# Output weight halved ahead of time: a two-layer decoder step on one core

## The chip, the cores and the metric

The kernel runs on one core of a Trainium2 chip. A core has five engines that run their own instruction streams: TensorE (PE in the profile, with its weight loads as PEld), VectorE (DVE), ScalarE (ACT), GpSimd (POOL) and SyncE (SP), which here only issues DMA transfers. The time is device microseconds (us) of one execution. One execution with the hardware profiler on gives the profile and the trace.

## The reference, cut to what matters

One inference step of a decoder with two layers, a Mamba-2 SSD layer and a multi-head latent attention (MLA) layer, for a prompt of 1024 tokens and 8 sample sequences of 8 tokens each, all in float32, model width 1024. The change is in the MLA layer.

```
def mla_sample_attn(q_nope, q_pe, ckv, kpe, pool_ckv, pool_kpe, layer, page_table, w_uk, w_uv):
    q_lat = absorb(q_nope, w_uk)
    stats = latent_partial(q_lat, q_pe, ckv, kpe, causal)
    def page_step(carry, pt):
        page = latent_partial(q_lat, q_pe, pool_ckv[layer, pt], pool_kpe[layer, pt], None)
        return merge_partial(carry, page), None
    (_, l, acc), _ = lax.scan(page_step, stats, page_table.T)
    return latent_out(l, acc, w_uv)

def mla_output(o, gate, w_out):
    gated = o.reshape(b, t, MLA_WIDTH) * jax.nn.silu(gate.astype(F32))
    return jnp.einsum('bte,ed->btd', gated.astype(gate.dtype), w_out)
```

The gate is a part of the layer's input projection. Each sample sequence has 2048 cached tokens in pages (a latent of 256 and a rotary key of 32 per token). After `mla_output` come the residual sum and a final RMSNorm. `w_out` is 1024 x 1024.

## The kernel before

Matrix products that must keep float32 accuracy are made from halves: a value x is held as hi, its rounding to the matmul's input type, and lo = x - hi, and a product is three matmuls, hi*hi, hi*lo, lo*hi. `split` (line 125) makes them: ScalarE casts hi, VectorE (or GpSimd) subtracts for lo.

The MLA layer goes through these stages.

- Gates (`gate_block`, line 970, eight blocks b of 128 columns, three token pieces each): weight block loaded by `load_w` (line 316), split by ScalarE and GpSimd, 24 matmuls a piece, ScalarE's Silu into `gt`, stored to DRAM as `g_d`. `gather_kpe` and `page_rows` run between them; the gathered rotary keys go to DRAM as two 2 MB stores `kpe_d`.
- Latent and query projections (`mla_kv`, `mla_cq`, `mla_q`).
- Prompt attention, 16 heads (`mla_heads`, line 1466). In the last head the sample attention's first eleven steps (`FLOW`) are mixed in, and `preload` (line 1582) loads two of the eight 128-row blocks of the output weight.
- Sample attention with the output projection (`mla_sample`, line 1844). `Sample.flow` (line 1790) walks over 32 steps n, called pages here: one step treats 512 cached tokens of one sequence (four pages of the cache). A step transposes the next cache rows (`turn`, matmuls ct), transposes the last probabilities (`turn_p`, pt), makes the scores (`scores`, seven matmuls sc, the last from the rotary keys tk), takes their maximum (mx, nm) and exponential (P) (`softmax`, line 1640) and multiplies the last probabilities with the cache rows (`values`, matmuls o, accumulated in ac). `halves` (line 1706) splits the next cache rows: ScalarE casts kvh, GpSimd subtracts kvl. Cache rows pgr come by GpSimd's indirect DMA four steps ahead, rotary keys tk by SP two steps ahead.
- `MlaOut` (line 1869) holds the output projection. `pieces` is a generator that yields after half an output tile's first matmuls; `flow` calls it from step 8 on, so that its matmuls fill TensorE between the pages.

The weight blocks kk are taken in the order `WORD`. Six more blocks are loaded by SP three at a time (`weight`, line 1879), and `weight_split` (line 1884) makes their halves in steps 2 to 7:

```
WSP = (2, 3, 4, 4, 5, 6, 6, 7)
WENG = (2, 0, 2, 0, 2, 0, 2, 0)
```

`WSP` gives the step of each block, `WENG` who subtracts, GpSimd (2) or VectorE (0): one cast of 128 x 1024 on ScalarE and four subtractions of 128 x 256. For each output tile `load` fetches the gated attention output `og` and `split` cuts it into oh and ol, one tile ahead.

The order of TensorE's and GpSimd's instructions in the head and sample stages is as written. ScalarE's, VectorE's and SP's order is made when the program is built, by a planner with its own model of times: it may move an instruction ahead of others that are not ready. `issue_after(x)` keeps the instructions written inside it behind x on x's engine. Each engine runs its queue in order, so an instruction that waits holds those behind it.

Of the kernel before, what the change touches and what calls it, by code (L numbers as in the profile page):

```python
# [16 lines left out]
D = 1024  # L17
# [950 lines left out]


def gate_block(k, wp, raws, b):  # L970
    with k.tc.issue_after(k.gts[5].ins) if b in (3, 4) else nullcontext():
        ws = kslices(load_w(k, wp, k.I["mla_w_in"][0][:, 800 + 128 * b : 928 + 128 * b], 8, 128, "wg", 3, raws,
                            eng=k.nc.gpsimd, sub=4), 8)
    gt = wp.tile([128, T], F32, tag="gt", name=f"gt{b}", bufs=2)

    def ev(ci, t0, n, p):
        k.gts.append(k.nc.scalar.activation(gt[:, t0 : t0 + n], p[:, :n], AF.Silu))
# [18 lines left out]
def mla_in(k, right, mid):  # L996
    tc, nc, I = k.tc, k.nc, k.I
    k.g_d = k.dram.tile([8, 128, T], F32, name="g_d")
    with ExitStack() as st:
# [17 lines left out]
        k.kvs = [k.cm.tile([128, 2, 64], F32R, name=f"kvs{x}") for x in "hl"]  # L1017
        gates = (None for b in range(2, 8) for _ in gate_block(k, wg, rw, b))
        with open_pool(tc, name="kg", bufs=1, side="right") as kg:
# [20 lines left out]
        wcq = load_cw(k, wq, rw, 0, 512, "cw")  # L1040
        mla_kv(k, sp, wkv)
        wk.close()
# [5 lines left out]

def mla_kv(k, sp, ws):
    nc, I = k.nc, k.I  # L1050
# [7 lines left out]
    for i, (t0, m) in enumerate(TILES):  # L1058
# [39 lines left out]
        if i < 8:  # L1098
            kh, kl = k.kT
            split(k, kh[64:96, t0 : t0 + m], kl[64:96, t0 : t0 + m], p[64:96, 256 : 256 + m])  # L1100


# [363 lines left out]
def mla_heads(k, hd, sm, early, st):  # L1466
# [8 lines left out]
    for h in range(MH):  # L1475
# [19 lines left out]
        for t in range(12):  # L1495
# [8 lines left out]
            if h + 1 == MH and t == 0:  # L1504
                sm.preload()
            if len(held) > LEAD:
# [45 lines left out]
class Sample:  # L1552
# [28 lines left out]

    def preload(self):
        k = self.k
        self.pre = ExitStack()
        pp = self.pre.enter_context(open_pool(k.tc, name="pre4", bufs=1))
        self.wraw = {}
        for kk in WORD[:2]:
            self.wraw[kk] = pp.tile([128, D], F32, name=f"w5p{kk}")
# [18 lines left out]
    def late_open(self, st):  # L1607
        self.pre.close()
# [10 lines left out]
    def load_tk(self, n):  # L1619
        k, nc = self.k, self.k.nc  # L1620
        tk = self.ep.tile([96, 4, 256], F32R, tag="tk", name=f"tk{n}", bufs=2)
        for j in range(3):
            src = k.kpe_d[j % 2][:, :, 128 * n : 128 * n + 256].rearrange("r c x -> c r x")
            with k.tc.issue_after(k.lastq.ins):
                nc.sync.dma_start(tk[32 * j : 32 * j + 32].bitcast(F32), src)
        for j in range(2):
# [13 lines left out]
    def softmax(self, name, s, n, old):  # L1640
# [9 lines left out]
        l = self.small(name, "l4", 1, 4)  # L1650
        nc.scalar.activation(P[:, :n], s, AF.Exp, bias=nm, scale=SCALE, accum_out=l)
        f = None
# [39 lines left out]
    def turn(self, n, c):  # L1692
# [6 lines left out]
        tl = self.ep.tile([128, 512], F32R, tag=f"cTl{c}", name=f"cTl{n}_{c}", bufs=2)  # L1699
        a = nc.scalar.copy(th, pt)  # L1700
        b = nc.vector.tensor_tensor(tl, pt, th.bitcast(F32), op=ALU.subtract)
        if self.out:
            self.out.pins = a, b
        self.cT[n, c] = (th, tl)
# [85 lines left out]
    def flow(self):  # L1790
        N = len(self.items)
        for n in range(-1, N + 1):
# [9 lines left out]
            if t:  # L1802
                self.turn(n + 1, 1)
                yield
            parts = [WORD[WSP.index(n) + x] for x in range(WSP.count(n))] if out else []
# [29 lines left out]
            if out:  # L1835
                if n in MORE:
                    next(out.fill, None)
                if n + 1 == OUT0[0]:
                    next(out.fill)
                    self.k.nc.sync.dma_start(out.fw, self.k.I["final_norm_w"].partition_broadcast(128))  # L1840
            yield


def mla_sample(k, sm, flow):
    with ExitStack() as st:
        psum = st.enter_context(open_pool(k.tc, name="ps4", bufs=1, space=PS))
        out = MlaOut(k, st, psum)
        sm.open(st, psum, out)
        out.raw = sm.wraw
        for kk in WORD[2:5]:  # L1850
            out.weight(kk)
        out.fill = fill = out.pieces(range(8))
        next(fill)
        for _ in flow:
            if not hasattr(sm, "accT") and not any(kk in out.raw for kk in WORD[:2]):
                sm.late_open(st)
        last = None
# [11 lines left out]
class MlaOut:  # L1869
    def __init__(self, k, st, psum):  # L1870
        tc, nc, I = k.tc, k.nc, k.I
# [3 lines left out]
        self.fw = sp.tile([128, D], F32, name="fw")  # L1875
        self.raw = {}
        self.ws = [[self.wp.tile([128, D], F32R, name=f"w5{x}{kk}", bufs=1) for x in "hl"] for kk in range(8)]

    def weight(self, kk):
        k, nc, wp = self.k, self.k.nc, self.wp  # L1880
        self.raw[kk] = self.sp.tile([128, D], F32, tag="h5", name=f"w5r{kk}", bufs=3)
        WQ(nc).dma_start(self.raw[kk], k.I["mla_w_out"][0][kk * 128 : kk * 128 + 128])

    def weight_split(self, kk, half):
        hi, lo = self.ws[kk]
        raw = self.raw[kk]
        nc, x = self.k.nc, WENG[WORD.index(kk)]
        if not half:
            with self.k.tc.issue_after(self.pins[0].ins):
                nc.scalar.copy(hi, raw)  # L1890
        for a in range(2 * half, 2 * half + 2):
            s = slice(256 * a, 256 * a + 256)
            with self.k.tc.issue_after(self.pins[1].ins):
                (nc.gpsimd if x & 2 else nc.vector).tensor_tensor(lo[:, s], raw[:, s], hi[:, s].bitcast(F32),
                                                                  op=ALU.subtract)
        if half:
            del self.raw[kk]
            if 2 <= WORD.index(kk) < 5:
                self.weight(WORD[WORD.index(kk) + 3])

    def pieces(self, tiles, src=None):
        k, nc, sp, ws = self.k, self.k.nc, self.sp, self.ws

        def load(i):
            t0, m = TILES[i]
            oh = sp.tile([128, 8, 128], F32R, tag="oh5", name=f"oh5{i}", bufs=2)
            ol = sp.tile([128, 8, 128], F32R, tag="ol5", name=f"ol5{i}", bufs=2)
            g = src
            if i < 8:
                g = sp.tile([128, 8, 128], F32, tag="og5", name=f"og5{i}", bufs=2)  # L1910
                nc.sync.dma_start(g, k.og_d[:, :, t0 : t0 + m].rearrange("b p t -> p b t"))
            return oh[:, :, :m], oh[:, :, 64:] if m == 64 else ol, g, oh

        queue = [load(tiles[0])]
        if tiles[0] == 0:
            yield
        split(k, *queue[0][:3], parts=4 if tiles[0] == 0 else 0)
        if tiles[0] == 0:
            yield
        for n, i in enumerate(tiles):  # L1920
            t0, m = TILES[i]
            oh, ol, _, o2 = queue.pop(0)
# [8 lines left out]
            for hf, c in enumerate(cs):  # L1931
# [3 lines left out]
                for j, _ in enumerate(mm_tok(nc, p, m, nw, [  # L1935
                        (oh[:, kk], ol[:, kk], o2[:, kk], ws[kk][0][:, c], ws[kk][1][:, c]) for kk in WORD])):
                    if j == (7 if src else 11) and nw == 512:
# [142 lines left out]
```

## Time and profile before

| | us |
|---|---|
| median of three runs (lowest, highest) | 1930.48 (1929.45, 1934.53) |
| the profiled execution | 1939.72 |
| its span, first to last instruction | 1937.9 |
| mean granted TensorE clock | 0.994 |
| TensorE busy | 1894.9 |

Slices of the page: TensorE's busy tenths are 9 nearly everywhere; the lower ones are at the change from the first to the second half of the SSD layer (776 to 824 us), at the start of the sample attention, and at the end. A busy TensorE in this profile is not TensorE at its peak, since matmuls overlap; the granted clock tells when it ran slower. Stretches of time are given in us from the span's start. In the list of waits the columns are who waited, for whom, us in total, times and the longest. In a group the number after the bar is busy time, then the mean of one in ns, then idle time before it. In a timeline row the first two numbers are start and duration; a bracket holds the idle time before it and who ended it.

### The profile page before, as it was taken

What the parts mean: (1) busy time and instruction counts of PE and PEld (TensorE: products, weight loads), DVE (VectorE), ACT (ScalarE), POOL (GpSimd) and SP (SyncE); (2) the same over time, 40 slices, a digit from 0 to 9 for tenths busy, and PEclk for the clock granted to TensorE, in tenths of its full rate; (3) what the DMA queues carried; (4) which work ended last, traced back from release to release, by engine and by line L of the source; (5) the groups of instructions that cost most, each with busy time, mean ns of one, the idle gap of its engine ahead of it and who ended that gap; (6) DMA issues with size and microseconds to landing.
All of it is one profiled execution on the core that took longest, in us unless ns stands there. A gap on an engine that the chain in (4) does not pass through costs nothing.

```text
span 1937.9 us, 33631 instructions
## 1 busy us (share of the span) xinstructions
PE 1894.9 (98%) x12023; PEld 1733.7 (89%) x12023; DVE 1209.1 (62%) x2500; ACT 1100.4 (57%) x2525; POOL 828.6 (43%) x1122
## 2 busy tenths in 40 slices
PE   9999999999999999899999999999999999899998
PEld 7999999999999999788788998998888888688887
DVE  5557676767676767755534114567877878766674
ACT  6467566666666766732214314436777777755552
POOL 2447555555655555443004222104333435854551
PEclk9999999999999999999999999999999999989999
DMA  5123323233333332644434342223111112645441
GB/s 166 50 78 90 94 80 100 82 106 87 93 89 92 89 93 88 202 145 172 168 109 127 114 163 86 72 96 92 48 47 43 53 42 82 212 142 155 156 128 39
DMA packets 181088, 202.02 MB, mean 104 GB/s; under 512 B 18829, under 2 KB 147609, under 8 KB 180537
## 3 DMA queue, kind: packets, MB, share of 16 engines
q1 hardware_dynamic: 175864, 180.08, 30.3%
q0 software_dynamic: 4976, 19.66, 3.0%
q8 instruction: 95, 1.56, 0.3%
q14 instruction: 73, 0.59, 0.1%
q10 hardware_dynamic: 80, 0.13, 0.0%
HBM read 146.52 MB, written 53.28 MB: 103 GB/s over the span
## 4 chain that ended last, share of the span: by engine, by line
PE 87%; DMA 4%; ACT 3%; DVE 3%; issue 1%; POOL 1%; SPq 0%; POOLq 0%; DVEq 0%; ACTq 0%
PE pj L86 24%; PE pz L98 7%; PE pq L98 6%; PE pob L98 5%; PE p L98 5%; PE poa L98 3%; PE py L638 3%; PE sc L86 3%; PE o L86 2%; PE sc L1376 2%; PE o L1439 2%; PE o L1441 2%; PE st L1408 2%; DMA M<-acs_d 2%; PE st L1409 2%; PE st L1410 2%
## 5 line engine op out<-in xcount | busy, mean ns | idle before, releaser
L86 PE MATMUL pj<-xl,wih 128*128 128x384 f32 (+1 forms) x768 | 255.4, 333 | 0.0
L86 PE MATMUL pj<-xh,wih 128*128 128x384 f32 (+1 forms) x768 | 252.9, 333 | 0.5 <-ACT raw L512 0.3
L86 PE MATMUL pj<-xh,wil 128*128 128x384 f32 (+1 forms) x768 | 252.9, 329 | 0.0
L1422 POOL TENSOR_TENSOR tl<-P,th 128x384 fp32r<-128x384 f32 (+1 forms) x96 | 90.6, 944 | 232.3 <-ACT P L1420 190.6
L526 DVE SCALAR_TENSOR_TENSOR acc<-raw,vec,acc 128x1112 f32<-128x1112 f32 x96 | 139.9, 1458 | 14.3 <-ACT acc L522 13.4
L98 PE MATMUL pz<-wih,xh 128*128 128x256 f32 x504 | 143.4, 288 | 2.5 <-ACT z L567 2.5
L86 PEld LDWEIGHTS pj<-xh,wih 128*128 128x128 f32 x768 | 143.8, 188 | 1.9 <-ACT xh L273 0.7
L86 PEld LDWEIGHTS pj<-xl,wih 128*128 128x128 f32 x768 | 144.5, 188 | 1.0
L86 PEld LDWEIGHTS pj<-xh,wil 128*128 128x128 f32 x768 | 144.4, 188 | 0.5
L98 PE MATMUL pz<-wil,xh 128*128 128x256 f32 (+1 forms) x504 | 139.6, 283 | 0.0
L1419 ACT ACTIVATE th<-st 128x512 fp32r<-128x512 f32 x192 | 94.6, 493 | 65.9 <-PE st L1415 50.3
L633 ACT ACTIVATE M<-M,tok 128x128 f32<-128x128 f32 (+1 forms) x288 | 91.0, 386 | 67.7 <-DVE M L629 67.2
L98 PE MATMUL pz<-wih,xl 128*128 128x256 f32 x448 | 128.9, 288 | 0.0
L1712 POOL TENSOR_TENSOR kvl<-pgr,kvh 128x256 fp32r<-128x256 f32 x128 | 96.5, 781 | 65.6 <-ACT kvh L1710 65.5
L133 DVE TENSOR_TENSOR wil<-wraw,wih 128x512 fp32r<-128x512 f32 x88 | 74.2, 849 | 40.7 <-ACT wih L127 34.0
L98 PEld LDWEIGHTS pz<-wih,xh 128*128 128x128 f32 x504 | 95.9, 190 | 3.5 <-ACT z L567 2.9
L1420 ACT ACTIVATE P<-st 128x512 f32<-128x512 f32 x192 | 93.5, 487 | 0.0
L98 PEld LDWEIGHTS pz<-wil,xh 128*128 128x128 f32 (+1 forms) x504 | 92.8, 184 | 0.3
L614 POOL TENSOR_TENSOR xdd<-xsT,tok 128x256 f32<-128x256 f32 x64 | 49.9, 779 | 90.2 <-ACT xsT L600 89.7
L98 PEld LDWEIGHTS pz<-wih,xl 128*128 128x128 f32 x448 | 85.3, 190 | 0.5
L1422 DVE TENSOR_TENSOR tl<-P,th 128x512 fp32r<-128x512 f32 x96 | 70.7, 737 | 19.5 <-ACT P L1420 19.3
L127 ACT CAST wih<-wraw 128x512 fp32r<-128x512 f32 x92 | 55.9, 616 | 43.9 <-PE pj L86 28.9
(834 smaller groups left out, 6295.1 us busy)
## 6 DMA issues: line engine op xcount, KB each, us to landing
wraw<-in_ssd_w_in SPq DMA_DIRECT2D x92, 256.0 KB
M<-acs_d SPq DMA_DIRECT2D x64, 256.0 KB
s<-in_state_ssm SPq DMA_DIRECT2D x32, 256.0 KB
y_d<-y SPq DMA_DIRECT2D x64, 128.0 KB
out_s_ssm<-s SPq DMA_DIRECT2D x32, 256.0 KB
wraw<-in_ssd_w_out SPq DMA_DIRECT2D x12, 512.0 KB
q_d<-qt SPq DMA_DIRECT2D x32, 192.0 KB
qp<-q_d SPq DMA_DIRECT2D x8, 768.0 KB
```

The lines of the kernel that those rows point to most:

```text
L86: nc.tensor.matmul(out, a, b, start=(i == 0), stop=(i == n - 1))
L98: nc.tensor.matmul(o, a, b, start=(j == 0), stop=(j == len(ops) - 1))
L127: k.cast = nc.scalar.copy(hi, src)
L133: return (eng or nc.vector).tensor_tensor(lo, src, hi.bitcast(F32), op=ALU.subtract)
L526: last = nc.vector.scalar_tensor_tensor(acc, raw[:, j : j + n], k.convw[j][:, blk : blk + 1], acc, op0=ALU.mult, op1=ALU.add)
L614: nc.gpsimd.tensor_tensor(v3(xdd), v3(xsT), hb(2), op=ALU.mult)
L633: nc.scalar.activation(M[:m, h, :m], M[:m, h, :m], AF.Exp, bias=tk[:, 0, 4 * g + h : 4 * g + h + 1])
L638: nc.tensor.matmul(py[:m, h * 64 : h * 64 + 64], M[:m, h, :m], xsT[:m, h * 64 : h * 64 + 64], start=True, stop=True)
L1419: nc.scalar.activation(th[:, :n], ps[:, :n], AF.Exp, scale=SCALE)
L1420: nc.scalar.activation(P[:, :n], ps[:, :n], AF.Exp, scale=SCALE)
L1422: eng.tensor_tensor(tl[:, :n], P[:, :n], th[:, :n].bitcast(F32), op=ALU.subtract)
L1712: nc.gpsimd.tensor_tensor(rl[:, j], raw[:, j], rh[:, j].bitcast(F32), op=ALU.subtract)
```

## The change

The halves of the output weight are made in the gates' stage: `stage_out`, a generator with sixteen steps, loads half a block (128 x 512), casts hi, subtracts lo, and stores both to a DRAM tensor `w5_d`. One step is taken after each gate piece from the third of block 2 on, sixteen in all. `mla_kv` asks for further steps, of which there are none left then. In the last head two blocks of `w5_d` (both halves, 1 MB each) are preloaded on SP's queue; the other six are loaded one per page in steps 2 to 7 by DMAs that ScalarE issues, each behind the exponential of the step before. `weight_split` and its pins are gone.

In `pieces` two output tiles are loaded at the start and the third when the second is cut; the loads of later tiles, of the residual rows h and of the final norm's weight are issued behind the latest load of rotary keys; the subtractions for ol (four of 128 x 256 a tile) stand behind the latest `nm`, the negated maximum. `accT` and `gs4` are allocated from the start beside the preloaded blocks.

```
-WSP = (2, 3, 4, 4, 5, 6, 6, 7)
-WENG = (2, 0, 2, 0, 2, 0, 2, 0)
+NPW = 2
+WSP = (2, 3, 4, 5, 6, 7)
...
-    k.nc.sync.dma_start(raw, src.rearrange("(k p) e -> p k e", p=128))
+    k.lastload = k.nc.sync.dma_start(raw, src.rearrange("(k p) e -> p k e", p=128))
...
+def stage_out(k, pool):
+    nc = k.nc
+    k.w5_d = k.dram.tile([8, 128, 2, D], F32, name="w5_d")
+    for n in range(16):
+        kk, s = WORD[n // 2], slice(512 * (n % 2), 512 * (n % 2) + 512)
+        t = pool.tile([128, 2, 512], F32, tag="w5s", name=f"w5s{n}", bufs=3)
+        with k.tc.issue_after(k.lastload.ins):
+            nc.sync.dma_start(t[:, 1], k.I["mla_w_out"][0][kk * 128 : kk * 128 + 128, s])
+        nc.scalar.copy(t[:, 0].bitcast(F32R), t[:, 1])
+        nc.vector.tensor_tensor(t[:, 1].bitcast(F32R), t[:, 1], t[:, 0], op=ALU.subtract)
+        nc.sync.dma_start(k.w5_d[kk][:, :, s], t)
+        yield
...
+        stage = stage_out(k, st.enter_context(open_pool(tc, name="w5s", bufs=1)))
...
+        def gate_steps():
+            for b in range(2, 8):
+                for ci, _ in enumerate(gate_block(k, wg, rw, b)):
+                    if b > 2 or ci > 1:
+                        next(stage, None)
+                    yield
...
+        for kk in WORD[:NPW]:
+            self.ws[kk] = pp.tile([128, 2, D], F32R, name=f"w5{kk}")
             with k.tc.issue_after(k.lastq.ins):
-                k.nc.sync.dma_start(self.wraw[kk], k.I["mla_w_out"][0][kk * 128 : kk * 128 + 128])
+                k.nc.sync.dma_start(self.ws[kk].bitcast(F32), k.w5_d[kk])
...
-        nc.scalar.activation(P[:, :n], s, AF.Exp, bias=nm, scale=SCALE, accum_out=l)
+        self.expi = nc.scalar.activation(P[:, :n], s, AF.Exp, bias=nm, scale=SCALE, accum_out=l)
...
-            for kk in parts:
-                out.weight_split(kk, 0)
+            if out and n >= 0:
+                out.weights(n)
             if 0 <= n < N:
                 self.scores(n)
                 self.weigh(n)
-            if parts:
-                out.pins = out.pins[0], self.nmi
-            for kk in parts:
-                out.weight_split(kk, 1)
...
-                    self.k.nc.sync.dma_start(out.fw, self.k.I["final_norm_w"].partition_broadcast(128))
+                    with self.k.tc.issue_after(self.lasttk.ins):
+                        self.k.nc.sync.dma_start(out.fw, self.k.I["final_norm_w"].partition_broadcast(128))
...
+    def weights(self, n):
+        k = self.k
+        for x in range(WSP.count(n)):
+            kk = WORD[NPW + WSP.index(n) + x]
+            with k.tc.issue_after(k.sm.expi.ins):
+                k.nc.scalar.dma_start(self.ws[kk].bitcast(F32), k.w5_d[kk])
...
         def load(i):
+            t0, m = TILES[i]
+            g = sp.tile([128, 8, 128], F32, tag="og5", name=f"og5{i}", bufs=2)
+            with k.tc.issue_after(k.sm.lasttk.ins) if i > 1 else nullcontext():
+                nc.sync.dma_start(g, k.og_d[:, :, t0 : t0 + m].rearrange("b p t -> p b t"))
+            return g
+
+        def halves(i, g):
...
+                nc.scalar.copy(a, g)
+                for j in range(4):
+                    s = slice(2 * j, 2 * j + 2)
+                    with k.tc.issue_after(k.sm.nmi.ins):
+                        nc.vector.tensor_tensor(b[:, s], g[:, s], a[:, s].bitcast(F32), op=ALU.subtract)
...
+            g = [load(0), load(1)]
             yield
+            cut = [halves(0, g.pop(0))]
             yield
...
-            nc.sync.dma_start(h[:m], k.h_d[t0 : t0 + m])
-            if n + 1 < len(tiles):
-                queue.append(load(tiles[n + 1]))
+            with k.tc.issue_after(k.sm.lasttk.ins):
+                nc.sync.dma_start(h[:m], k.h_d[t0 : t0 + m])
...
                 if hf == 0:
                     if n + 1 < len(tiles):
-                        split(k, *queue[0][:3], parts=4 if tiles[n + 1] < 8 else 0)
+                        cut.append(halves(tiles[n + 1], g.pop(0)))
+                    if n + 2 < len(tiles):
+                        g.append(load(tiles[n + 2]))
```

More of the change, by code (lines that the diff above doesn't have):

```diff
@@ L1017, in mla_in @@
         k.kvs = [k.cm.tile([128, 2, 64], F32R, name=f"kvs{x}") for x in "hl"]
-        gates = (None for b in range(2, 8) for _ in gate_block(k, wg, rw, b))
+        def gate_steps():
[4 more added lines that the diff above has]
+                    yield
+        gates = gate_steps()
         with open_pool(tc, name="kg", bufs=1, side="right") as kg:
@@ L1046, in mla_in, with mla_kv @@
         mla_cq(k, sp, wcq)
-def mla_kv(k, sp, ws):
+def mla_kv(k, sp, ws, stage):
     nc, I = k.nc, k.I
@@ L1100, in mla_kv @@
             split(k, kh[64:96, t0 : t0 + m], kl[64:96, t0 : t0 + m], p[64:96, 256 : 256 + m])
+        next(stage, None)
 def mla_cq(k, sp, ws):
@@ L1580, in pt, with preload @@
         return self.psum.tile([128, 512], F32, tag=tag, name=name, bufs=bufs)
-    def preload(self):
+    def preload(self, st):
         k = self.k
[L1584 to L1588, printed above, removed]
+        pp = st.enter_context(open_pool(k.tc, name="pre4", bufs=1))
+        self.ws = {}
+        for kk in WORD[:NPW]:
+            self.ws[kk] = pp.tile([128, 2, D], F32R, name=f"w5{kk}")
             with k.tc.issue_after(k.lastq.ins):
-                k.nc.sync.dma_start(self.wraw[kk], k.I["mla_w_out"][0][kk * 128 : kk * 128 + 128])
+                k.nc.sync.dma_start(self.ws[kk].bitcast(F32), k.w5_d[kk])
     def load_cn(self, b):
@@ L1699, in turn @@
         tl = self.ep.tile([128, 512], F32R, tag=f"cTl{c}", name=f"cTl{n}_{c}", bufs=2)
[L1700 to L1703, printed above, removed]
+        split(k, th, tl, pt)
         self.cT[n, c] = (th, tl)
@@ L1804, in flow @@
                 yield
-            parts = [WORD[WSP.index(n) + x] for x in range(WSP.count(n))] if out else []
-            for kk in parts:
-                out.weight_split(kk, 0)
+            if out and n >= 0:
+                out.weights(n)
             if 0 <= n < N:
@@ L1846, in mla_sample @@
         psum = st.enter_context(open_pool(k.tc, name="ps4", bufs=1, space=PS))
-        out = MlaOut(k, st, psum)
+        out = MlaOut(k, st, psum, sm)
         sm.open(st, psum, out)
-        out.raw = sm.wraw
-        for kk in WORD[2:5]:
-            out.weight(kk)
+        sm.late_open(st)
+        k.sm = sm
         out.fill = fill = out.pieces(range(8))
         next(fill)
-        for _ in flow:
-            if not hasattr(sm, "accT") and not any(kk in out.raw for kk in WORD[:2]):
-                sm.late_open(st)
+        drain(flow)
         last = None
@@ L1875, in __init__ @@
         self.fw = sp.tile([128, D], F32, name="fw")
[L1876 to L1899, printed above, removed]
+        self.ws = dict(sm.ws)
+        for kk in WORD[NPW:]:
+            self.ws[kk] = self.wp.tile([128, 2, D], F32R, name=f"w5{kk}", bufs=1)
+    def weights(self, n):
[4 more added lines that the diff above has]
+                k.nc.scalar.dma_start(self.ws[kk].bitcast(F32), k.w5_d[kk])
     def pieces(self, tiles, src=None):
@@ L1905, in load @@
             t0, m = TILES[i]
+            g = sp.tile([128, 8, 128], F32, tag="og5", name=f"og5{i}", bufs=2)
[4 more added lines that the diff above has]
+            t0, m = TILES[i]
             oh = sp.tile([128, 8, 128], F32R, tag="oh5", name=f"oh5{i}", bufs=2)
             ol = sp.tile([128, 8, 128], F32R, tag="ol5", name=f"ol5{i}", bufs=2)
[L1908 to L1915, printed above, removed]
+            a, b = oh[:, :, :m], oh[:, :, 64:] if m == 64 else ol
+            if src:
+                split(k, a, b, g)
+            else:
+                nc.scalar.copy(a, g)
[3 more added lines that the diff above has]
+                        nc.vector.tensor_tensor(b[:, s], g[:, s], a[:, s].bitcast(F32), op=ALU.subtract)
+            return a, b, oh
+        if src is None:
+            g = [load(0), load(1)]
             yield
-        split(k, *queue[0][:3], parts=4 if tiles[0] == 0 else 0)
-        if tiles[0] == 0:
+            cut = [halves(0, g.pop(0))]
             yield
+        else:
+            cut = [halves(tiles[0], src)]
         for n, i in enumerate(tiles):
             t0, m = TILES[i]
-            oh, ol, _, o2 = queue.pop(0)
+            oh, ol, o2 = cut.pop(0)
             h = sp.tile([128, D], F32, tag="h5", name=f"h5{i}", bufs=3)
-            nc.sync.dma_start(h[:m], k.h_d[t0 : t0 + m])
-            if n + 1 < len(tiles):
-                queue.append(load(tiles[n + 1]))
+            with k.tc.issue_after(k.sm.lasttk.ins):
+                nc.sync.dma_start(h[:m], k.h_d[t0 : t0 + m])
             ss = sp.tile([128, 4], F32, tag="ss5", name=f"ss5{i}", bufs=2)
```

11 lines of the change are left out of this document (5 added, 6 removed).

## The prediction

> **What bounds the kernel now.** I read the page first, then busy time by stretches, then the waits of one stretch, then its timeline by engine.
>
> ```profile
> PE 1894.9 (98%) x12023; PEld 1733.7 (89%) x12023; DVE 1209.1 (62%) x2500; ACT 1100.4 (57%) x2525; POOL 828.6 (43%) x1122
> ...
> 1071.00:1150.00 79.00, 78.77 (x493) 78.33 (x492) 6.99 (x15) 17.98 (x33) 16.62 (x24) 1.00 0.34 127
> 1667.60:1717.70 50.10, 37.52 (x207) 32.83 (x206) 38.14 (x76) 30.90 (x59) 34.71 (x44) 0.83 0.76 242
> 1717.70:1891.50 173.80, 173.80 (x1034) 150.56 (x1033) 111.49 (x244) 93.17 (x204) 90.97 (x114) 1.00 0.43 137
> 1891.50:1937.90 46.40, 38.46 (x233) 33.25 (x231) 23.17 (x60) 12.42 (x29) 7.29 (x11) 0.95 0.10 32
> ```
>
> The first line is busy time of each engine over the span. In the others the columns are the stretch, its length, busy time of PE, weight loads, DVE, ACT and POOL, the granted clock, DMA share and GB/s. TensorE is busy for 98% of the span, so only idle TensorE time and a low clock can be won. The gates (1071 to 1150) and the pages with output tiles between them (1717.7 to 1891.5) leave nothing. The stretch from 1667.6 to 1717.7, pages 3 to 8 of the sample attention, leaves 12.6 us idle, at a clock of 0.83. There stand the splits of the output weight. Who is waited for:
>
> ```profile
> PE pt L1739 <- ACT P L1651: 4.2, 2, 3.8
> PE pt41n L1678 <- ACT P41n L1651: 3.2, 1, 3.2
> PE o L86 <- DVE ac L1760: 3.1, 1, 3.1
> PE o L86 <- DVE pTl L133: 2.0, 2, 1.1
> ...
> 1674.00:1678.00 4.00, 3.04 (x25) 2.91 (x25) 4.00 (x7) 2.31 (x5) 3.81 (x6) 1.00 1.09 370
> 1690.00:1694.00 4.00, 1.72 (x6) 1.45 (x7) 4.00 (x8) 0.00 (x0) 3.81 (x6) 0.65 0.61 201
> 1706.00:1710.00 4.00, 4.00 (x15) 3.42 (x14) 1.95 (x4) 2.78 (x4) 2.81 (x4) 0.50 0.69 254
> ```
>
> All four waits (12.5 us of the 12.6) are for ScalarE or VectorE work of the softmax chain. VectorE is busy for the whole of 1674 to 1678 and 1690 to 1694, and after the idle time TensorE runs at half clock (0.50). What those engines do there beside the attention:
>
> ```profile
> L1894 POOL TENSOR_TENSOR w5l<-w5r,w5h 128x256 fp32r<-128x256 f32 x12 | 9.1, 781 | 0.0
> L1894 DVE TENSOR_TENSOR w5l<-w5r,w5h 128x256 fp32r<-128x256 f32 x12 | 8.7, 775 | 0.0
> L1890 ACT CAST w5h<-w5r 128x1024 fp32r<-128x1024 f32 x6 | 6.1, 1048 | 0.0
> ...
> L1894 DVE TENSOR_TENSOR w5l<-w5p,w5h 128x256 fp32r<-128x256 f32 x4 | 3.9, 1023 | 0.0
> L1894 POOL TENSOR_TENSOR w5l<-w5p,w5h 128x256 fp32r<-128x256 f32 x4 | 2.8, 729 | 2.2 <-PE ct L1697 2.2
> L1890 ACT CAST w5h<-w5p 128x1024 fp32r<-128x1024 f32 x2 | 2.1, 1053 | 0.0
> ```
>
> So 12.6 us of VectorE, 8.2 of ScalarE and 11.9 of GpSimd are splits: of VectorE's 38.14 us a third.
>
> **The splits leave (gain).** What six pages cost without them is bounded by two kinds of page:
>
> ```profile
> 1667.34 0.39 PE L86 MATMUL sc<-tk,qpr 96*128 96x512 f32 x1
> 1672.68 0.39 PE L86 MATMUL sc<-tk,qpr 96*128 96x512 f32 x1
> 1672.91 0.17 PE L86 MATMUL sc41n<-kvsh,qlh 128*128 128x8 f32 x1
> 1673.61 0.37 PE L86 MATMUL o<-kvh,pTh 128*128 128x256 f32 x1
> 1684.74 0.69 PE L1687 MATMUL o41n<-cn,pn 8*128 8x256 f32 x2
> 1725.40 0.39 PE L86 MATMUL sc<-tk,qpr 96*128 96x512 f32 x1
> 1725.63 0.40 PE L98 MATMUL p<-w5h,oh 128*128 128x512 f32 x1
> 1728.39 0.28 PE L86 MATMUL o<-kvh,pTh 128*128 128x256 f32 x1
> 1732.68 0.40 PE L86 MATMUL sc<-tk,qpr 96*128 96x512 f32 x1
> ```
>
> The last score matmul marks a page. From page 9 to 10 TensorE never waits: 1732.68 - 1725.40 = 7.28 us, of which twelve output matmuls take 1728.39 - 1725.63 = 2.76; a page is 4.52 us of TensorE work. That is the floor. From page 2 to 3, where no page has its full share of splits yet, it is 1672.68 - 1667.34 = 5.34 us, TensorE waiting a little for the chain score, maximum, exponential, transpose. Pages 3 to 8 also hold two sets of first scores (1673.61 - 1672.91 = 0.70 each) and one first accumulation (0.69): 2.1 us. So six pages take 6 x 4.52 + 2.1 = 29.2 to 6 x 5.34 + 2.1 = 34.1 us, against 50.1. I take 5.0 a page, 32.1 us: without filler between them the chain stays visible, but page 2 to 3 still holds one cast of 1.05 us. Gain 18.0 us, bounds 16.0 and 20.9. The clock's part is in it, since the floor was measured at full clock, and with gaps under 1 us a page it should stay there. Late next is the same chain, at about 0.5 us a page.
>
> **Weight slices on ScalarE's queue (cost inside that gain, and a risk).** Six triggers stand in ScalarE's order after an exponential. The trace has one trigger of that queue, and on SP both a quick case and a held one:
>
> ```profile
> 1669.94 1.49 SPq L1882 DMA_DIRECT2D w5r<-in_mla_w_out  x3
> 1673.44 3.24 SPq L1625 DMA_DIRECT2D tk<-kpe_dh  x1
> 1933.83 0.56 ACTq L1972 DMA_DIRECT2D out_y_sample<-h  x1
> ```
>
> 0.5 us each, 3 us in all, is less than the 8.2 us of casts that go; I count it as inside the 5.0. The bound above is 3.24 us each, 19.4 in all, what SP's queue was held with the three of the first row and more loads before it. Behind a held trigger wait the cache cast, the transposes' casts and the next exponential, and TensorE for them. I take the low end, since ScalarE's queue would hold one or two slices at a time.
>
> **Bytes.** A slice is 128 x 2 x 1024 x 4 B = 1.05 MB, a page's cache rows 0.52 MB, its rotary keys 0.20: 1.77 MB a page. At the 370 GB/s of the row of 1674 to 1678 that is 4.8 us, under 5.0 but only just. The two output tiles, the final norm's weight and the sample gates (1.8 MB) add 4.9 us once: 6 x 4.8 + 4.9 = 33.7 us, 1.6 above my 32.1. The last slice is wanted only in page 9, so half of this shows: +0.8. The two preloaded halves make one 1.05 MB more at the start of the last head (2.8 us at that rate). Behind it on SP stand page 2's keys (next fence), not used until 1667.34: nothing.
>
> **Output tiles.** Loads move behind the latest keys, subtractions behind the maximum.
>
> ```profile
> 1645.68 1.18 SPq L1625 DMA_DIRECT2D tk<-kpe_dh  x1
> 1678.35 1.05 ACT L127 CAST oh<-og 128x1024 fp32r<-128x1024 f32 x1 [0.74 <-DMA og<-og_d]
> 1687.14 3.55 DVE L131 TENSOR_TENSOR ol<-og,oh 128x256 fp32r<-128x256 f32 x4
> ```
>
> Before, the second tile's four subtractions held VectorE for 3.55 us ahead of the work that TensorE then waited 3.1 us for (the accumulation). Now only the first tile falls in the stretch, its subtractions after page 7's maximum, where half a tile of filler is about to start. Its cast may wait for its load as before, 0.74 us. I count +1.0 for the tile, 0 to 5.7 (below). Two tiles ahead instead of one, and residual rows after the keys, have a whole page of slack while TensorE is full: nothing; if they came late, a half tile's add would wait, and TensorE with it.
>
> **The staging in the gates (cost).** Sixteen steps: load 256 KB, cast, subtract, store 512 KB.
>
> ```profile
> L133 DVE TENSOR_TENSOR wil<-wraw,wih 128x512 fp32r<-128x512 f32 x88 | 74.2, 849 | 40.7 <-ACT wih L127 34.0
> L127 ACT CAST wih<-wraw 128x512 fp32r<-128x512 f32 x92 | 55.9, 616 | 43.9 <-PE pj L86 28.9
> ...
> ACT gt L977 <- PE pj L86: 44.0, 14, 4.0
> ...
> 1117.95 0.32 SPq L1533 DMA_DIRECT2D kpe_dh<-kpeh  x1
> 1129.30 0.95 POOL L1235 MEMSET kTh<- 2x1024 f32 x1 [13.08 <-DMA kpe_dl<-kpel]
> ```
>
> ScalarE gets 16 x 0.616 = 9.9 us on top of 17.98 of 79, VectorE 16 x 0.849 = 13.6 on top of 6.99; transfers 12.6 MB, 34 us at 370 GB/s, on top of 0.34 x 79 = 27: 61 of 79. SP gets 32 more triggers of 0.32 us. All lies under TensorE's 78.77. The cover goes only where a cast waits for its load ahead of a gate's activation: ScalarE stands idle 44.0/14 = 3.1 us before each of those, so a wait up to 3.1 us costs nothing. The worst is a load behind the two key stores (1117.95 to 1129.30, 11.35 us): 8.2 us of TensorE, once. I take +1, near the low end, bounds 0 and 8.2. A gain has no place: TensorE idles for 0.2 us there.
>
> **Sum.** -18.0 + 0.8 + 1.0 + 1.0 = -15.2 us, made against the profiled execution, 1939.72 us (span 1937.9 and 1.8 around it), which lies 9.2 us over the median of the three runs shown, 1930.48. Subtracted from the median: 1915.3, so 1915. Ends: pages -20.9 to -16.0, tile 0 to 5.7, staging 0 to 8.2, bytes 0 to 1.6: -20.9 to -0.5, 1910 to 1930.
>
> **Rivals.**
> First, the transfers become the bound, or the first tile loses to the slices. In one microsecond (1680 to 1681) the two busy queues passed:
>
> ```profile
> q0 software_dynamic: 89, 0.36, 88.7%
> q1 hardware_dynamic: 88, 0.05, 14.8%
> ```
>
> Packets, MB, share: as many packets each, but seven times the bytes for the queue with the larger ones. A slice's rows are 8 KB, a tile's 512 B, so two slices in flight (2.1 MB, 5.7 us at 370 GB/s) would pass ahead of the tile, and ScalarE could hold its cast for 5.7 us. At 300 GB/s, or with that hold, the stretch takes 38 to 41 us: -15.2 shrinks to about -8, 1922. For it: a page's bytes need 4.8 of 5.0 us. Against: before, DMA was as full from 1674 to 1678, and the cast waited 0.74 us.
> The Trainium skill (DMA: Bandwidth & Descriptors, Queues, rings and completion order) says that each DMA engine goes round robin between queues, switching only at packet boundaries. By that rule the stretch loses up to 5.7 us, and the sum would be -9.5 or 1921; shared by bytes it would be half of that, 1918; the trace's 89 against 88 packets agrees with the rule.
> Second, slower: ScalarE's triggers are held as SP's was. It decides from 15.2/6 = 2.5 us more each; at 3.24 instead of 0.5 it costs 16.4 us, 1932; at a page's 4.8 us of transfers it would be 25.8 us, 1941. For it: the held row and full DMA. Against: the other SP triggers at 0.5.
> Third, the staging holds ScalarE behind the key stores: +8.2 for one cast, 1922; two such casts, 1930, no change. For it: loads and stores share SP's queue. Against: TensorE's slack of 3.1 us at each gate.
> Fourth, the change does not do what it says: pages stay slow for another cause. Against: the waits name the very engines that the splits fill; only a page period above 8 us would say so, and page 2 to 3 had 5.34.
>
> **How the numbers follow.** The forecast has 0.64 (own range 1909 to 1921), the first rival 0.10 (all faster), the second 0.15 (0.12 slower, 0.03 no change), the third 0.09 (0.04 faster, 0.03 no change, 0.02 slower), the fourth 0.02 (half no change, half slower). About 0.3%, 5.8 us, is what a measurement of this kernel can tell. Faster 0.78, same 0.07, slower 0.15. The range 1909 to 1931 leaves out about 0.05 below and 0.13 above.
>
> **What would show it.** Right: score matmuls of pages 2 to 8 about 5 us apart, clock 1.00 throughout, no wait over 1 us for P or the accumulation, first output matmul about 16 us earlier, TensorE idle near 0 in the gates. Wrong: ACT trigger rows of 2 us or more; a cast of a tile or of a staged half waiting for its DMA while TensorE waits for ScalarE; a clock of 0.5 between 1660 and 1700; gates longer than 79 us.

## The result and the profile after

| | us |
|---|---|
| before, median of 21 runs | 1931.43 |
| after, median of 21 runs | 1936.05 |
| after / before | 1.0025, 95% interval 1.0017 to 1.0032 |
| profiled execution after, its span | 1935.3, 1933.5 |

The change makes the kernel 4.6 us slower, a little under what I called the limit of telling; the interval excludes a gain. Before's first profile (1939.72) was an unusual execution, 8.3 us over its median, so a second one is used below.

The page of the changed kernel, and busy time by stretches (columns as before). The stretch runs from the last score matmul of page 2 to that of page 8, the next two rows:

```profile
PE 1892.9 (98%) x12023; PEld 1730.5 (90%) x12023; DVE 1207.1 (62%) x2500; ACT 1100.7 (57%) x2533; POOL 818.5 (42%) x1106
```
```profile
1670.95:1712.36 41.41, 32.10 (x207) 27.46 (x206) 24.27 (x59) 23.67 (x53) 22.73 (x29) 0.92 0.87 296
```
```profile
1670.95 0.39 PE L86 MATMUL sc<-tk,qpr 96*128 96x512 f32 x1
...
1712.36 0.39 PE L86 MATMUL sc<-tk,qpr 96*128 96x512 f32 x1
```

The splits did leave: VectorE is busy for 24.27 us in the six pages, GpSimd for 22.73. But the pages take 41.4 us, not 32. TensorE's waits in 1660 to 1715 and its timeline with ScalarE's and SP's:

```profile
PE pt L1758 <- ACT P L1673: 8.6, 3, 7.8
```
```profile
1674.01 0.41 ACTq L1897 DMA_DIRECT2D w<-w_d  x1
1674.57 0.59 ACTq L1897 DMA_DIRECT2D w<-w_d  x1
1676.62 0.60 ACT L127 CAST cTh<-ct 128x512 fp32r<-128x512 f32 x1
1686.10 1.04 ACT L1917 CAST oh<-og 128x1024 fp32r<-128x1024 f32 x1 [8.87 <-DMA og<-og_d]
1687.05 0.68 ACT L1673 ACTIVATE P<-sc,nm 128x512 f32<-128x512 f32 x1
...
1674.02 1.83 SPq L1906 DMA_DIRECT2D og<-og_d  x2
...
1687.88 1.11 PE L1758 MATMUL pt<-ident,P 128*128 128x128 f32 x4 [7.82 <-ACT P L1673]
```

This is one stall. The slices of steps 2 and 3 are triggered together (1674.01 and 1674.57), and the planner put the first output tile's cast ahead of page 3's exponential (the row at 1687.05; experiment 1's text calls it page 4's). The tile was issued at 1674.02 and is not there before 1686.10; ScalarE holds 8.87 us, TensorE 7.82. The other pages have a period of 5.1 to 6.1 us. While everything waits, the transfers run (stretches with clock, DMA share and GB/s last):

```profile
1681.00:1682.00 1.00, 0.00 (x0) 0.00 (x0) 0.00 (x0) 0.00 (x0) 0.00 (x0) 1.00 1.07 439
1684.00:1685.00 1.00, 0.00 (x0) 0.00 (x0) 0.00 (x0) 0.00 (x0) 0.00 (x0) 0.50 0.99 369
```

The queues of two stretches (packets, MB, share), 1680 to 1682 and then 1684 to 1686:

```profile
q10 hardware_dynamic: 74, 0.61, 71.5%
q0 software_dynamic: 63, 0.22, 26.6%
q1 hardware_dynamic: 75, 0.04, 6.3%
...
q1 hardware_dynamic: 724, 0.36, 65.7%
q0 software_dynamic: 95, 0.32, 42.0%
```

q10 is ScalarE's queue with the slices, q0 the cache rows, q1 SP's with the tiles. While a slice is under way each queue gets about as many packets (74, 63, 75), but the tile's are of 0.5 KB: 0.04 MB in 2 us. When the slices are through, q1 moves 0.36 MB in 2 us. The Trainium skill (DMA: Bandwidth & Descriptors, Queues, rings and completion order) says that the engines take turns between queues by packets; these rows agree.

The other loss is ahead of the pages. TensorE's waits from 1043 to 1090 (before had one of 0.2 us there):

```profile
PE pj L86 <- ACT gt L991: 2.1, 2, 1.5
PE xtp L268 <- DVE hl L274: 1.4, 1, 1.4
```
```profile
1048.75 2.45 DVE L979 TENSOR_TENSOR w5s<-w5s 128x512 fp32r<-128x512 f32 x2
...
1051.79 0.55 PE L268 MATMUL xtp<-ident,xt 128*128 128x128 f32 x3 [1.42 <-DVE hl L274]
...
1074.88 0.80 SPq L996 DMA_DIRECT2D g_d<-gt  x2
...
1079.53 4.77 SPq L977 DMA_DIRECT2D w5s<-in_mla_w_out  x3
...
1084.47 0.87 ACT L991 ACTIVATE gt<-pj 128x384 f32<-128x384 f32 x2 [7.40 <-DMA g_d<-gt]
1085.01 0.42 PE L86 MATMUL pj<-hh,wgh 128*128 128x320 f32 x1 [1.50 <-ACT gt L991]
```

Seven of the sixteen staged casts ran before 1071, in the norm that precedes the gates, where ScalarE and VectorE make the halves of the layer's input: the planner took the steps earlier than the code has them. A pair of staged subtractions (2.45 us) then stands ahead of an input half. And a gate's activation waits 7.40 us for an earlier gate's store to DRAM to free its buffer. That store was issued at 1074.88, ahead of the 256 KB loads of the staging that then hold SP (4.77 us for three). What ran beside it was the gather of the rotary keys (q0 here). The load of the gather's indices stands on SP directly behind a staged store and comes at 1070.94, 31.7 us after the norm's transpose at 1039.21; in before's second profile that is 18.1 us, and its gather runs ahead of the gates' stores. The two rows, and the queues from 1077 to 1080:

```profile
1070.94 0.67 SPq L1540 DMA_DIRECT2D kpidx<-in_page_table  x1
1073.87 1.15 POOL L1542 DMA_INDIRECT kprows<-in_cache_kpe,kpidx  x1 [0.71 <-DMA kpidx<-in_page_table]
...
q0 software_dynamic: 64, 1.05, 82.5%
q1 hardware_dynamic: 48, 0.21, 16.8%
```

How much of the 7.40 us is the gather's and how much the staging's own transfers', no run separates. Between 1040 and 1120 the changed kernel loses 4.4 us against both profiles of before.

### The profile page after: what moved, and what is told of

It is laid out like the page before. It is cut to its first block, busy times and chain, and to the rows that moved or that the text cites. A ratio compares the mean times of both kernels' runs of the same rounds, so it can differ in the third digit from the quotient of the medians.

```text
span 1933.5 us, 33666 instructions
## 1 busy us (share of the span) xinstructions
PE 1892.9 (98%) x12023; PEld 1730.5 (90%) x12023; DVE 1207.1 (62%) x2500; ACT 1100.7 (57%) x2533; POOL 818.5 (42%) x1106
## 4 chain that ended last, share of the span: by engine, by line
PE 87%; DMA 4%; ACT 3%; DVE 3%; issue 1%; POOL 1%; SPq 0%; ACTq 0%; POOLq 0%; DVEq 0%
PE pj L86 22%; PE pz L98 8%; PE pq L98 6%; PE pob L98 5%; PE p L98 5%; PE poa L98 4%; PE py L638 3%; PE sc L86 3%; PE o L86 2%; PE sc L1400 2%; PE o L1463 2%; PE o L1465 2%; PE st L1432 2%; PE st L1433 2%; PE st L1434 2%; PE o L1464 2%
## 5 line engine op out<-in xcount | busy, mean ns | idle before, releaser
L98 PE MATMUL p<-w,oh 128*128 128x512 f32 (+3 forms) x304 | 88.7, 385 | 0.6 <-DVE h L1949 0.6
L614 POOL TENSOR_TENSOR xdd<-xsT,tok 128x256 f32<-128x256 f32 x64 | 50.1, 782 | 89.1 <-ACT xsT L600 88.6
```

The costliest lines, as they stand in the source:

```text
L98: nc.tensor.matmul(o, a, b, start=(j == 0), stop=(j == len(ops) - 1))
L614: nc.gpsimd.tensor_tensor(v3(xdd), v3(xsT), hb(2), op=ALU.mult)
```

## The experiments

All ran against before; medians are of the experiment's own runs. Numbers are those that the expectations use; there is no 7. The runs were taken in groups, and before's median moved between them: 1931.43 beside the change, 1932.23 beside experiments 1 to 3, 1932.85 beside 4, 5, 6 and 8, 1932.93 beside 9 and 10. So a difference of medians from two groups is uncertain by up to 1.5 us; taken against each group's own before, the 5.2 us of staging below are 6.0, the 7.3 of experiment 4 are 7.9, the 6.6 of experiment 5 are 5.2, the 3.5 of experiment 6 are 4.9, and the 4.9 of experiment 8 are 5.5.

**Before again.** No edit.

> The kernel before once more, to see how much of its stall in pages 3 to 8 is in every execution. Theory A (the profiled execution of before, 1939.7 us against a median of 1931.4, had an unusual stall in the pages): a time near 1931, and the stretch from page 2's last score matmul to page 8's about 8 us shorter than the 50.1 us of the first profile, so about 42. Theory B (profiling itself, or another stage, made it longer): a time near 1939, or the same 50 us in that stretch.

Measured: 1932.01, near the median. Busy time by stretch, page 2 to page 8 again:

```profile
1664.20:1709.78 45.58, 36.95 (x207) 31.50 (x206) 38.00 (x77) 30.94 (x59) 35.73 (x45) 0.85 0.77 241
```

45.6 us, not 50.1. Half of theory A's 8 us: 4.5 us of the stall that I set out to win belonged to one execution. The other 3.4 lay ahead of the norm (1037.32 against 1040.68 for the same transpose), where the change touches nothing.

**Experiment 1: the tiles' cast pinned.**

```
-                nc.scalar.copy(a, g)
+                with k.tc.issue_after(k.sm.expi.ins):
+                    nc.scalar.copy(a, g)
```

> The changed kernel with each output tile's cast on ScalarE kept behind the latest exponential (page 7's for the first tile, instead of ahead of page 4's). Theory A (the 7.82 us wait of TensorE at 1687.88 is this cast, which waits 8.87 us for its tile behind two weight slices): the wait goes, and the time falls by 6 to 8 us against the changed kernel, to 1928 to 1930. Theory B (transfers are the bound there): something else waits for the same transfers, rotary keys or cache rows, and the time falls by 3 us at most, 1933 to 1936.

Measured: 1936.82; 1.0019 of before (1.0007 to 1.0031). The 7.82 us wait is gone, the time is not: theory B, a little over its range. Waits of TensorE (1660 to 1715), the stretch, and the triggers' line with the semaphore waits ahead of them (ns min/median/max):

```profile
PE o L86 <- ACT pTh L127: 3.2, 3, 2.0
PE sc L86 <- DMA tk<-kpe_dh: 2.9, 1, 2.9
```
```profile
1670.91:1712.76 41.85, 34.26 (x206) 29.35 (x205) 22.00 (x53) 22.39 (x50) 23.82 (x31) 0.92 0.92 300
```
```profile
L1897 ACTq EVENT_SEMAPHORE  x8: 17/28/6559, 1673.9 to 1704.9; - x8
L1897 ACTq DMA_DIRECT2D w<-w_d x6: 326/327/387, 1673.9 to 1705.0; - x6
```
```profile
1699.88 0.33 ACTq L1897 DMA_DIRECT2D w<-w_d  x1
1700.24 0.59 ACT L127 CAST cTh<-ct 128x512 fp32r<-128x512 f32 x1 [5.87 <-issue]
```

Rotary keys come late (2.9 us), and ScalarE is held by its own triggers after all: not in the trigger's row (0.33 us) but in a semaphore wait ahead of it, 6.56 us before 1699.88. Two more rows tell what such waits end with:

```profile
1688.97 0.59 ACT L127 CAST cTh<-ct 128x512 fp32r<-128x512 f32 x1 [2.54 <-DMA og<-og_d]
...
1699.95 0.47 PE L86 MATMUL sc<-tk,qpr 96*128 96x512 f32 x1 [2.85 <-DMA tk<-kpe_dh]
```

The first stands right behind a trigger (1688.55): the cast reads no output tile, yet ScalarE stood until one had landed. The second is page 6's score matmul; its wait for the keys ends 0.07 us after the trigger's. I read both as a trigger that waits until an earlier transfer, issued by SP, has landed; why it waits for that one, no trace here shows. The pin also costs time behind the stretch: from page 8's last score matmul to page 9's it is 9.24 us, in the change 8.01.

**Experiments 2 and 3: nearly no staging, without and with the pin.**

```
-    for n in range(16):
+    for n in range(2):
...
-                    if b > 2 or ci > 1:
+                    if b == 7 and ci > 0:
...
-                k.nc.scalar.dma_start(self.ws[kk].bitcast(F32), k.w5_d[kk])
+                k.nc.scalar.dma_start(self.ws[kk].bitcast(F32), k.w5_d[WORD[0]])
```

> The changed kernel with two of the sixteen staging steps only, at the end of the gates, and all slices read from that one block, so the output projection's result is left out while every later transfer keeps its size. Theory A (staging costs the 4.4 us by which the changed kernel fell behind from the norm before the gates to their end): 1931 to 1932, and TensorE not idle for VectorE's halves in the norm or for ScalarE's gates. Theory B (that loss is from something else, since casts and subtractions lie under TensorE's work): 1935 to 1937.

> Both edits at once: the tile's cast pinned and two staging steps only (the projection's result left out as before). If the two losses are separate they add: 1924 to 1927 from 1936. If the bound in the pages is transfers, it stays at 1930 to 1933.

Measured: 1930.81, 0.9994 of before (0.9985 to 1.0004), and 1930.90, 0.9989 (0.9979 to 0.9999). The staging costs 1936.05 - 1930.81 = 5.2 us, and with the pin 1936.82 - 1930.90 = 5.9: theory A. The losses do not add: the time is the same with the pin and without it. The pin shortens the stretch from 41.3 (experiment 2) to 39.1 us, and page 8 to 9 grows from 8.0 to 9.4. Both profiles are of the shortest execution of each kernel (1926.99 and 1926.39, about 4 us under the medians). The stretch of experiment 3, with DMA at 0.95:

```profile
1663.24:1702.32 39.08, 32.49 (x206) 27.61 (x205) 21.20 (x53) 21.46 (x48) 22.77 (x30) 0.96 0.95 318
```

**Experiment 4: as 3, with slices of half the size.**

```
-                k.nc.scalar.dma_start(self.ws[kk].bitcast(F32), k.w5_d[WORD[0]])
+                k.nc.scalar.dma_start(self.ws[kk][:, 0].bitcast(F32), k.w5_d[WORD[0]][:, 0])
...
-  ws[kk][:, 0, c], ws[kk][:, 1, c]) for kk in WORD
+  ws[kk][:, 0, c], ws[kk][:, int(kk in WORD[:NPW]), c]) for kk in WORD
```

> The third experiment's kernel (cast pinned, two staging steps only) with the six late slices cut to their hi half, which stands for both halves in the output's matmuls (so the projection's result is left out again): 3.1 MB fewer to load, same triggers, same work on every engine. Theory A (from 1674 to 1704 the transfers are the bound: DMA share 1.0 there, 9 to 10 MB at 308 to 337 GB/s): 3.1 MB at those rates are 9 to 10 us, so from page 2's last score matmul to page 8's it takes 31 to 33 us instead of 39.1, at full clock, with no wait for the rotary keys, and the time is 5 to 8 us under the third experiment's 1930.9. Theory B (ScalarE's triggers or the order of its queue are the bound, not the bytes): the stretch stays at 37 to 39 us and the time at 1929 to 1931.

Measured: 1923.64, 0.9946 (0.9923 to 0.9969), 7.3 us under experiment 3.

```profile
1668.56:1700.97 32.41, 30.81 (x206) 26.38 (x205) 21.33 (x52) 21.19 (x48) 22.84 (x30) 1.00 0.94 290
```

The same instructions, 3.1 MB fewer, and the stretch falls by 6.7 us to 32.4 at full clock, with no wait of TensorE for the keys. Theory A: the bytes are the bound. The two profiled executions differ by 1.3 us only, since that of experiment 3 reaches page 2 5.3 us earlier (1663.24 against 1668.56), ahead of anything that the edit touches. The DMA share is still 0.94, so the share alone does not tell whether transfers hold the kernel up; the waits and the length do.

**Experiment 5: the second tile and the sample gates later.**

```
-            g = [load(0), load(1)]
+            g = [load(0)]
             yield
             cut = [halves(0, g.pop(0))]
+            g.append(load(1))
...
-            with k.tc.issue_after(k.sm.lasttk.ins) if i > 1 else nullcontext():
+            with k.tc.issue_after(k.sm.lasttk.ins) if i > 0 else nullcontext():
...
+        with k.tc.issue_after(self.lasttk.ins):
             nc.sync.dma_start(gs, ...)
```

> The changed kernel with two transfers taken out of the crowded stretch: the second output tile is loaded only after the first is cut, and the sample gates' 0.26 MB of 256-byte pieces behind the last rotary keys. Cast order is the change's. Theory A (transfers bound the stretch, and the first tile waits behind all that is in flight): the tile's wait of 8.9 us falls by the 0.77 MB and their small pieces, 2 to 4 us, and the time to 1932 to 1934. Theory B (the cast waits for the two slices alone): no difference, 1935.5 to 1937.

Measured: 1942.68, 1.0054 (1.0035 to 1.0073). Neither time: 6.6 us slower than the change. ScalarE's rows:

```profile
1686.93 1.04 ACT L1918 CAST oh<-og 128x1024 fp32r<-128x1024 f32 x1 [9.71 <-DMA og<-og_d]
...
1716.43 1.04 ACT L1918 CAST oh<-og 128x1024 fp32r<-128x1024 f32 x1 [8.52 <-DMA og<-og_d]
```

The first tile is no earlier, and the second tile, issued at 1700.84 among the last slices, now makes a second hold, since its cast too stood ahead of a transpose's cast. So the hold hangs on the slices, and a cast that is not pinned pays it for every tile loaded beside them. Taking 0.77 MB away could not help the first tile, for in the change all of it is issued behind that tile on the same queue (1674.02 and 1675.91): while the two slices run, from 1678 to 1682, the queue passes 118 packets in the change and 120 here, and in the next 2 us 695 and 807. The wait is thus theory B's, on the slices alone; why it is 0.8 us longer stays open. The profiled execution (1948.11) is one of the four longest of ten (1947.98 to 1951.52, where the other six took 1942.82 at most), so the second hold may be shorter in the others.

**Experiment 6: staging kept out of the norm.**

```
-        nc.scalar.copy(t[:, 0].bitcast(F32R), t[:, 1])
+        with k.tc.issue_after(k.gts[-1].ins):
+            nc.scalar.copy(t[:, 0].bitcast(F32R), t[:, 1])
...
-                    if b > 2 or ci > 1:
+                    if b > 3 or (b == 3 and ci > 1):
```

> The changed kernel with the staging steps' casts kept behind the latest gate activation and begun one block later, with the last steps between the latent projections, so that none of it falls into the norm. Theory A (the 5.2 us that the staging costs come from steps that the planner put into the norm, 1.4 us at the token transposes, and from loads mixed with the gates' weight loads, 2.3 us): the norm's loss of 2 us goes, and at least part of the gates', 1932 to 1934. Theory B (the cost is that of 12.6 MB of transfers and 48 more triggers wherever they are): no difference, 1935 to 1937.

Measured: 1932.59, 0.9988 (0.9974 to 1.0002): 3.5 us of the 5.2 are back, theory A. From the norm's transpose to the last gate activation it is 108.1 us, as in before's second profile (108.0); the change takes 112.4. The gather stands ahead of the gates' stores again (1062.97 against 1072.70). TensorE's waits from 1043 to 1300:

```profile
PE pq L98 <- ACT qt L1169: 1.4, 1, 1.4
PE qs L1356 <- DMA qp<-q_d: 0.3, 1, 0.3
PE pj L86 <- ACT gt L992: 0.2, 1, 0.2
```

The norm's and the gates' waits are gone; one of 1.4 us has come in the query projection.

**Experiment 8: as 1, slices on SP's queue.**

```
-            with k.tc.issue_after(k.sm.expi.ins):
-                k.nc.scalar.dma_start(self.ws[kk].bitcast(F32), k.w5_d[kk])
+            with k.tc.issue_after(k.sm.lasttk.ins):
+                k.nc.sync.dma_start(self.ws[kk].bitcast(F32), k.w5_d[kk])
```

> The first experiment's kernel (cast pinned) with the six slices issued on SP's queue behind the latest rotary keys, not on ScalarE's. Theory A (ScalarE was held by triggers that wait for an earlier transfer to complete, 6.56 us ahead of 1699.88): ScalarE is not held, pages 2 to 8 take 32 to 34 us and the time falls by 3 to 5 us to 1932 to 1934. Theory B (the transfers are the bound, whoever issues them): the same 37 us, or longer because rotary keys queue behind slices on SP, and 1936 to 1940.

Measured: 1931.91, 0.9987 (0.9973 to 1.0001), 4.9 us under experiment 1. Between the theories: the time is A's, the stretch (38.2 us) is not.

```profile
PE sc L86 <- DMA tk<-kpe_dh: 5.6, 2, 3.2
```
```profile
1667.36:1705.57 38.21, 30.97 (x207) 26.10 (x205) 24.62 (x56) 23.54 (x52) 26.19 (x34) 1.00 0.94 312
```

No trigger holds ScalarE any more and the clock is full, but the rotary keys now queue behind three slices on SP.

**Experiments 10 and 9: the edits together.** 10 is 6 and 8, with the pin one exponential earlier. 9 is 10 with transfers placed by need (the pin's lines below are in both):

```
-WSP = (2, 3, 4, 5, 6, 7)
+WSP = (2, 3, 5, 5, 7, 7)
...
-            g = [load(0), load(1)]
+            g = [load(0)]
             yield
             cut = [halves(0, g.pop(0))]
+            g.append(load(1))
...
-            with k.tc.issue_after(k.sm.lasttk.ins) if i > 1 else nullcontext():
+            with k.tc.issue_after(k.sm.lasttk.ins) if i > 0 else nullcontext():
...
-                with k.tc.issue_after(k.sm.expi.ins):
+                with k.tc.issue_after(k.sm.expw.ins):
                     nc.scalar.copy(a, g)
...
+        with k.tc.issue_after(self.lasttk.ins):
             nc.sync.dma_start(gs, ...)
...
+                if n == OUT0[0]:
                     with self.k.tc.issue_after(self.lasttk.ins):
                         self.k.nc.sync.dma_start(out.fw, ...)
```

> Three edits together: staging out of the norm (as in the sixth experiment), the six slices on SP's queue (as in the eighth), each tile's cast on ScalarE behind the exponential before the latest. If the two gains measured singly, 3.5 and 4.1 us against the changed kernel's 1936.05, are separate, they add: 1927 to 1930. If the slower staging kept the pages' transfers apart by chance, 1931 to 1933.

> As the other kernel of this call, with transfers moved by their need: slices two by two behind the rotary keys (pages 2, 3, 5, 5, 7, 7), the second tile loaded when the first is cut, the final norm's weight a page later and the sample gates behind the last keys: 1.3 MB leave the stretch from page 2 to page 8, and no key stands behind more than two slices. If bytes bound the stretch, 1.3 MB at 310 GB/s are 4 us: pages 2 to 8 in 33 to 35 us without waits for keys, 1923 to 1927. If the last two slices then come too late for the first output tile, TensorE waits in page 9 and it is 1927 to 1931.

Measured: 1926.56, 0.9971 (0.9959 to 0.9983); and 1921.80, 0.9949 (0.9934 to 0.9963): 9 beats both kernels. Both times lie just under the better range that was expected. In 10 the stretch is 36.3 us, with 3.7 us of TensorE waiting for the keys; the stretch of 9 and all of TensorE's waits from 1660 to 1715:

```profile
1666.58:1698.35 31.77, 30.52 (x207) 26.47 (x205) 22.58 (x56) 21.06 (x48) 21.91 (x28) 1.00 0.92 317
```
```profile
PE pt L1760 <- issue: 0.7, 2, 0.5
PE pt L1760 <- ACT P L1675: 0.6, 2, 0.4
```

31.8 us at full clock, with no wait of TensorE for a transfer. Which of the four moves of 9 gained how much, no run separates.

## Why the prediction was wrong, by its steps

- **What bounds it.** The waits named were real, but the stretch of 50.1 us came from an execution that I had seen to lie 9.2 us over the median, and I took its whole stall as there to be won. The second profile has 45.6.
- **The splits leave.** Right for the engines' work: 32.1 us forecast for the six pages; 32.4 where the bytes are fewer (experiment 4), 31.8 where they are placed well (9).
- **Bytes: the step that failed.** I put 33.7 us of transfers against 32.1 and counted 0.8 us. The amount was right (33.7 us x 370 GB/s = 12.5 MB; experiment 3 has 39.08 x 318 = 12.4 MB). The rate was a peak: 370 GB/s of a 4 us window, where the mean over experiment 3's stretch is 318 with DMA 0.95 busy. The forecast's 12.5 MB at 318 GB/s are 39.2 us, the length of that stretch; halving the slices took 6.7 us out. My own row of 1667.6 to 1717.7 held the rate: 242 GB/s at a DMA share of 0.76 would be 318 at a full share. The price was 7 us where 0.8 stood. The rival "transfers become the bound" had the stretch at 38 to 41 us and a chance of 0.10; its time, 1922, was still 14 us too low, since it too started from the 50.1 us and took +1 for the staging.
- **The first tile.** I took 1.0 us, with 5.7 as the most. ScalarE waited 8.87 us, TensorE 7.82: my bound was the two slices at 370 GB/s. Beside the cache rows they were under way until after 1682, 8 us from their issue, and most of the tile's packets came only then. That is not on top of the bytes: with the pin the same microseconds turned up at the triggers and the keys (a stretch of 41.85 against 41.41).
- **Triggers.** The rows are quick, as taken (0.33 to 0.59 us). That a wait can stand ahead of the row, until an earlier transfer has landed, I did not see; in the change ScalarE's semaphore waits there are 38 ns at most, in experiment 1 up to 6.56 us. Slices on SP gave 4.9 us back, so the second rival's place was right, its price per trigger was not.
- **Staging.** +1 forecast, 0 to 8.2 as bounds; 5.2 measured. The sign and the bounds hold, the place does not: not a load behind the key stores, but steps moved into the norm, and a gate's buffer not yet stored. The slack of 3.1 us before each activation covered only part of that: one activation waited 7.40 us, and the norm's input halves (1.42 us of TensorE) have no such slack.
- **The rest.** The forecast was 18.0 gained for 2.8 of costs. In the one pair of profiles (before again, after) the norm and gates lose 4.4, the pages gain 45.6 - 41.4 = 4.2, and 3.1 more are lost elsewhere, 1.9 of it ahead of the norm, where before's own two profiles differ by 3.4. Against the forecast that is 4.5 us of stall that the first profile alone had, 7.5 in the pages (41.4 where I had 32.1 + 0.8 + 1.0), 3.4 in the staging (4.4 where I had 1) and the 3.1: 18.5 in all, which turn -15.2 into +3.3, the difference of the two spans (1933.5 and 1930.2). By medians the change without staging is about 1 us faster than before (0.9994), so the pages' net gain may be nearer 1 us than 4; which, these runs leave open.

## What to carry to other kernels

When work is moved off the engines by loading its result, add up the bytes of the stretch and divide by a mean rate taken over as long a stretch, never by the best few microseconds. If that comes near the time that the engines need, it is the forecast, and the order of the transfers decides who stalls: keep compute engines from waiting on them, by issuing large loads from a queue with no compute behind it and by placing them by need. Pinning a cast behind the work that is due first only moved the wait here (1936.05 and 1936.82). And look at where a planner can move added work, not only at where the code puts it; a profile that lies well above the median is taken again before its stall is counted as a gain.

## What was not expected of the hardware

- VectorE's subtraction of a staged half took 0.68 us when GpSimd was idle, and 1.2 each (2.45 for two at 1048.75) beside GpSimd's subtractions, which also took longer than the 0.80 us of before:

```profile
1048.37 1.07 POOL L133 TENSOR_TENSOR ck2l<-wraw,ck2h 128x288 fp32r<-128x288 f32 x1 [2.41 <-ACT ck2h L127]
1049.41 1.25 POOL L133 TENSOR_TENSOR ck3l<-wraw,ck3h 128x288 fp32r<-128x288 f32 x1
```

The Trainium skill (SBUF — State Buffer, SBUF: two separate sides) says that a VectorE operation with two SBUF inputs and a GpSimd operation that reads SBUF take one shared port in turns; the staged subtraction has both inputs in SBUF, and the rows agree: the two and the two together take 2.83 us (1048.37 to 1051.20), one after another they would take 2 x 0.68 + 2 x 0.80 = 2.96. No run here took the overlap away alone.

- A 512 KB tile of 0.5 KB pieces, issued at 1674.02, was there at 1686.10, 12 us later, while 1 MB slices of 8 KB rows went by.
